# One input buffer of a fused layer norm and GELU: loaded in one transfer instead of four row transfers

## The chip, the cores and the metric

The kernel runs on one core of a Trainium2 chip. The metric is the device time of one execution in microseconds (us). Some executions of a kernel are over 1.5% slower than its fastest; they are said to be slow. A profile's span is some 1.8 us shorter than the time of the same execution, so times are compared with times and places in a profile with places in a profile.

Ratios are the mean time of one kernel's fast runs over that of the other's of the same rounds, so they are not quite the ratio of the medians that are quoted beside them. For the experiments, working them out again from the recorded times gives the ratios only if the first run of each list is left out. That run is the profiled one; it is counted in the medians.

## The reference

The input is 8192 rows of 2048 numbers in fp32, 67.1 MB. The output has the same size.

```python
mean = np.mean(x, axis=-1, keepdims=True)
var = np.var(x, axis=-1, keepdims=True)
normalized = (x - mean) / np.sqrt(var + eps)
out = gamma * normalized + beta
return 0.5 * out * (1 + np.tanh(np.sqrt(2 / np.pi) * (out + 0.044715 * out ** 3)))
```

## The kernel before

The rows are cut into 16 buffers (`B`) of 128 partitions with four rows each (`R`), 4.19 MB a buffer. There are five slots in SBUF (`SLOTS`). A buffer is loaded into a slot, overwritten there by its result and stored from there. SP, the sync engine, issues all loads, and before each it waits until the slot's former buffer has been stored. The engines wait for each other by semaphores, counters that one raises and another waits for; a transfer that has landed adds 16, or the multiple of it that the program asks for. The rows of one partition are contiguous in memory, so a whole buffer moves in runs of 32 KB, one for each partition, and a row transfer in runs of 8 KB.

```python
@block.sync
def _(sy):
    for b in range(B):
        s = slot(b)
        if stored(b):
            sy.wait_ge(s_store[s], stored(b))
        for q in range(R):
            if b == 0:
                sy.dma_start(out=xts[s][:, q:q + 1], in_=xg[0, :, q:q + 1]).then_inc(s_first[q], 16)
            elif b == SPLIT:                                   # SPLIT = 3
                sy.dma_start(out=xts[s][:, q:q + 1], in_=xg[b, :, q:q + 1]).then_inc(s_load[s], 16)
        if b not in (0, SPLIT):
            sy.dma_start(out=xts[s], in_=xg[b]).then_inc(s_load[s], 16 * R)
```

The vector engine (DVE) takes the statistics of each row. The first of a buffer waits for the load. In the order of its instructions the statistics of the next row come ahead of the scaling of this one:

```python
def stats(s, q, wait, count):
    ...
    for j in range(nsub):
        ins = ve.bn_stats(out=sts[:, q, j, :], in_=xr[:, j, :])
        if j == 0 and wait:
            ins._wait_ge(*wait)
            ...
...
for k in range(SLOTS * R):
    s, q = divmod(k, R)
    stats(s, q, (s_load[s], 16 * R) if q == 0 else None, k + 1)
    scale((q - 1) % R, k + 1)
```

The scalar engine (ACT) normalizes each row and later applies GELU to it, and it issues the stores: whole buffers, except for the last, which goes out row by row.

```python
ins = ac.activation(out=xt[:, q], in_=pss[i % 2], func=ACT.Gelu_apprx_tanh)._wait_ge(s_t, i + 1)
if by_row(b):                                                  # b == B - 1
    ins.then_inc(s_r, 1)
    ac.dma_start(out=og[b, :, q:q + 1], in_=xt[:, q:q + 1])._wait_ge(
        s_r, b + q + 1).then_inc(s_store[slot(b)], 16)
    ac.sem_inc(s_g, 1)
elif q == R - 1:
    ins.then_inc(s_r, 1)
    ac.dma_start(out=og[b], in_=xt)._wait_ge(s_r, b + 1).then_inc(s_store[slot(b)], 16)
    ...
```

Of the kernel before, what the change touches and what calls it, by code (L numbers as in the profile page):

```python
# [9 lines left out]

R = 4
SLOTS = 5
SPLIT = 3
K = 16


# [1 line left out]
def kernel(  # L18
# [19 lines left out]
    xg = xf.rearrange("(b p r) d -> b p r d", p=P, r=R)  # L38
# [8 lines left out]
    def sb(name, shape, dt):  # L47
        return pool.tile(shape, dt, name=name)

    xts = [sb(f"xt{s}", [P, R, d], f32) for s in range(SLOTS)]  # L50
# [17 lines left out]
    def sem(name):  # L68
        return tc.alloc_semaphore(name)

    s_first = [sem(f"first{q}") for q in range(R)]
    s_load = [sem(f"load{s}") for s in range(SLOTS)]
# [16 lines left out]
    def slot(b):  # L89
        return (b + SLOTS - 1) % SLOTS  # L90

    def row(p):
        return rows[p:p + 1, :, :d // K]

    def split(v):
        return v.rearrange("o (k f) -> o k f", k=K)
# [7 lines left out]
    def stored(b):  # L104
        return sum(16 * (R if by_row(c) else 1) for c in range(b) if slot(c) == slot(b))

    with tc.tile_critical(no_gpsimd_drain=True):  # L107
        with nc.Block(no_gpsimd_drain=True) as block:
# [7 lines that stand above are left out]
                    for q in range(R):  # L116
                        if b == 0:
                            sy.dma_start(out=xts[s][:, q:q + 1], in_=xg[0, :, q:q + 1]).then_inc(s_first[q], 16)
                        elif b == SPLIT:
                            sy.dma_start(out=xts[s][:, q:q + 1], in_=xg[b, :, q:q + 1]).then_inc(s_load[s], 16)  # L120
                    if b not in (0, SPLIT):
                        sy.dma_start(out=xts[s], in_=xg[b]).then_inc(s_load[s], 16 * R)

            @block.gpsimd
            def _(po):
# [18 lines left out]
            @block.vector  # L144
            def _(ve):
                def stats(s, q, wait, count):
                    xr = xts[s][:, q].rearrange("p (s f) -> p s f", f=FMAX)
                    for j in range(nsub):
                        ins = ve.bn_stats(out=sts[:, q, j, :], in_=xr[:, j, :])  # L149
                        if j == 0 and wait:  # L150
                            ins._wait_ge(*wait)
                            if wait[0] is s_load[s]:
                                ins.then_inc(s_load[s], -16 * R)
                    ins.then_inc(s_o, 1)
                    ve.bn_aggr(out=mvs[:, q], in_=sts[:, q])._wait_ge(s_o, count).then_inc(s_a, 1)  # L155

                def scale(q, count):
                    ve.tensor_tensor(out=zgs[q % 2], in0=yks[q % 2], in1=g_t,  # L158
                                     op=ALU.mult)._wait_ge(s_n, count).then_inc(s_z, 1)

                ve.memset(b_hl, 0.0).then_inc(s_m, 1)  # L161
                for q in range(R):
                    stats(slot(0), q, (s_first[q], 16), q + 1)
                    if q == 0:

                        ve.tensor_tensor(out=split(b_hl[32:33]), in0=row(32), in1=split(b_hl[32:33]),  # L166
                                         op=ALU.subtract)._wait_ge(s_c, 2).then_inc(s_m, 1)
                        ve.wait_ge(s_c, 3)
                    else:
                        scale(q - 1, q)  # L170
                ve.sem_inc(s_o, -R)
                ve.sem_inc(s_n, -(R - 1))
                with ve.Fori(0, (B - 1) // SLOTS):
                    for k in range(SLOTS * R):
                        s, q = divmod(k, R)
                        stats(s, q, (s_load[s], 16 * R) if q == 0 else None, k + 1)
                        scale((q - 1) % R, k + 1)
                    ve.sem_inc(s_o, -SLOTS * R)
                    ve.sem_inc(s_n, -SLOTS * R)
                scale(R - 1, 1)  # L180
# [102 lines left out]
```

## Time and profile before

| what | before |
|---|---|
| time, median of 3 (range) | 319.97 us (319.55 to 320.1) |
| span of the profile | 318.3 us |
| moved by DMA | 134.26 MB, mean 422 GB/s |
| stores issued in the steady part | every 19.36 us |
| last row store issued at | 309.36 us |

The first line below is from the page of the kernel before and gives busy time, share of the span and number of instructions of each engine (PE is the matmul engine, PEld its weight loads, POOL the GpSimd engine, which finishes the statistics of each row). The other two are from its lists of waits: who waited for whom, total us, how often, and the longest.

```profile
PE 244.3 (77%) x520; PEld 57.1 (18%) x520; DVE 247.3 (78%) x386; ACT 251.7 (79%) x132; POOL 110.4 (35%) x201
...
DVE sts L149 <- DMA xt<-in_x_dram: 31.2, 11, 3.8
...
SPq L122 <- DMA out_dram<-xt: 241.2, 11, 47.9
```

No engine is near its limit. The waits say that DVE waits for loads and that the loads wait for stores, which looks like a chain that could be shortened. (The "page" of a kernel is the summary of its profile.)

### The profile page before, as it was taken

The numbers are of one execution on the slowest core, as the hardware profiler recorded it, in microseconds if no ns is written. First come the engines' busy times: TensorE is split into PE (matmuls) and PEld (weight loads), VectorE is DVE, ScalarE is ACT, GpSimd is POOL, SyncE is SP. The second block draws the span as 40 slices with busy tenths as digits, with TensorE's granted clock in tenths as the row PEclk, the third lists the DMA queues.
The fourth block names the chain that finished last, engine by engine and source line by source line (L and its number), as shares of the span: only waits on it lengthen the run. The fifth ranks groups of instructions, "written<-read, shape, count | busy, mean of one in ns | idle before, by whom it ended". The sixth has DMA issues, their size and how long they took to land.

```text
span 318.3 us, 2090 instructions
## 1 busy us (share of the span) xinstructions
PE 244.3 (77%) x520; PEld 57.1 (18%) x520; DVE 247.3 (78%) x386; ACT 251.7 (79%) x132; POOL 110.4 (35%) x201
## 2 busy tenths in 40 slices
PE   2769999999999989687796868959689596877850
PEld 1212222222212112111121112212112111211110
DVE  3499999999999898786968968699686987869710
ACT  2769999999999989698696977969599595986860
POOL 1144444444444444232442333343342442324300
DMA  7999999999999999999999999999999999999994
GB/s 287 441 453 406 389 433 436 441 416 449 420 436 445 413 449 416 445 428 432 449 408 453 416 449 424 432 449 412 453 416 445 428 428 445 420 445 424 436 401 204
DMA packets 6002, 134.26 MB, mean 422 GB/s; under 512 B 704, under 2 KB 752, under 8 KB 752
## 3 DMA queue, kind: packets, MB, share of 16 engines
q1 hardware_dynamic: 3168, 67.11, 49.5%
q10 hardware_dynamic: 2832, 67.13, 49.0%
q14 instruction: 2, 0.02, 0.0%
HBM read 67.13 MB, written 67.11 MB: 422 GB/s over the span
## 4 chain that ended last, share of the span: by engine, by line
DMA 64%; ACT 14%; DVE 10%; POOL 5%; PE 3%; issue 1%; ACTq 0%; DVEq 0%; POOLq 0%; SPq 0%
DMA out_dram<-xt 31%; DMA xt<-in_x_dram 31%; ACT yk L195 9%; DVE sts L149 7%; ACT xt L202 4%; POOL ves L135 3%; DVE zg L158 2%; PE ps L220 2%; DMA rows<-in_gamma_dram 2%; POOL rss L137 2%; POOL nms L139 1%; DVE mvs L155 1%; PE ps L237 1%; ACT g_t L191 1%; ACTq L205 0%
## 5 line engine op out<-in xcount | busy, mean ns | idle before, releaser
L149 DVE BATCH_NORM_STATS2 sts<-xt 128x6 f32<-128x512 f32 x256 | 157.7, 679 | 33.0 <-DMA xt<-in_x_dram 31.2
L195 ACT ACTIVATE yk<-xt,nms,rss 128x2048 bf16<-128x2048 f32 x64 | 133.8, 2090 | 47.9 <-POOL nms L139 41.9
L237 PE MATMUL ps<-zg,ident 128*128 128x512 bf16 x256 | 120.8, 627 | 54.8 <-DVE zg L158 53.8
L233 PE MATMUL ps<-b_hl,ones_b 33*128 33x512 bf16 x256 | 120.6, 624 | 2.2 <-PEq L228 2.2
L202 ACT ACTIVATE xt<-ps 128x2048 f32<-128x2048 f32 x64 | 119.0, 1859 | 1.5 <-PE ps L237 1.5
L135 POOL TENSOR_SCALAR ves<-mvs 128x1 f32<-128x1 f32 x64 | 38.4, 600 | 178.4 <-DVE mvs L155 178.4
L158 DVE TENSOR_TENSOR zg<-yk,g_t 128x2048 bf16<-128x2048 bf16 x64 | 76.4, 1194 | 19.2 <-ACT yk L195 19.2
L237 PEld LDWEIGHTS ps<-zg,ident 128*128 128x128 bf16 x256 | 27.6, 130 | 148.0 <-DVE zg L158 112.7
L233 PEld LDWEIGHTS ps<-b_hl,ones_b 33*128 33x128 bf16 x256 | 27.0, 127 | 92.1 <-issue 88.4
L139 POOL TENSOR_SCALAR nms<-mvs,rss 128x1 f32<-128x1 f32 x64 | 35.7, 558 | 6.3
L137 POOL TENSOR_TENSOR rss<-ves,mhalf 128x1 f32<-128x1 f32 x64 | 35.3, 552 | 5.3
L155 DVE BATCH_NORM_AGGREGATE mvs<-sts 128x2 f32<-128x24 f32 x64 | 16.9, 264 | 2.2
L220 PE MATMUL ps<-rows,ones 1*128 1x512 f32 x8 | 7.2, 1076 | 6.1 <-DMA rows<-in_gamma_dram 6.1
L188 ACT ACTIVATE b_hl<-rows 1x2048 bf16<-1x2048 f32 x1 | 1.9, 1910 | 5.2 <-DMA rows<-in_beta_dram 5.2
L166 DVE TENSOR_TENSOR b_hl<-rows,b_hl 1x2048 bf16<-1x2048 f32 x1 | 2.3, 2282 | 2.5 <-ACT b_hl L189 2.5
L220 PEld LDWEIGHTS ps<-rows,ones 1*128 1x128 f32 x8 | 2.5, 326 | 9.2 <-DMA rows<-in_gamma_dram 6.1
L191 ACT ACTIVATE g_t<-ps 128x2048 bf16<-128x2048 f32 x1 | 1.9, 1878 | 2.1 <-PE ps L220 2.1
L184 ACT ACT_TABLE_LOAD x1 | 1.3, 1283 | 0.9 <-SPq L107 0.9
L189 ACT ACTIVATE b_hl<-rows 1x2048 bf16<-1x2048 f32 x1 | 1.9, 1908 | 0.0
L161 DVE MEMSET b_hl<- 33x1024 uint32 x1 | 0.9, 912 | 1.2 <-SPq L107 1.2
L126 POOL MEMSET ones<- 65x128 f32 x1 | 0.2, 202 | 0.5 <-SPq L107 0.5
L130 POOL TENSOR_SCALAR_AFFINE_SELECT ident<-ident 128x128 bf16<-128x128 bf16 x1 | 0.3, 295 | 0.1
(7 smaller groups left out, 0.9 us busy)
## 6 DMA issues: line engine op xcount, KB each, us to landing
out_dram<-xt ACTq DMA_DIRECT2D x15, 4096.0 KB, 33.3
xt<-in_x_dram SPq DMA_DIRECT2D x14, 4096.0 KB
xt<-in_x_dram SPq DMA_DIRECT2D x8, 1024.0 KB, 8.2
out_dram<-xt ACTq DMA_DIRECT2D x4, 1024.0 KB, 9.0
rows<-in_beta_dram ACTq DMA_DIRECT2D x2, 8.0 KB, 5.8
rows<-in_gamma_dram ACTq DMA_DIRECT2D x1, 8.0 KB, 5.1
```

The costliest lines, as they stand in the source:

```text
L135: po.tensor_scalar(out=ves[:, c], in0=mvs[:, k, 1:2], scalar1=float(eps), scalar2=1.0, op0=ALU.add, op1=ALU.mult)._wait_ge(s_a, k + 1).the ...
L137: po.tensor_tensor(out=rss[:, c], in0=ves[:, c], in1=mhalf, op=ALU.pow)._wait_ge(s_q, 2 * k + 1).then_inc(s_q, 1)
L139: po.tensor_scalar(out=nms[:, c], in0=mvs[:, k, 0:1], scalar1=rss[:, c], scalar2=-1.0, op0=ALU.mult, op1=ALU.mult)._wait_ge(s_q, 2 * k + 2 ...
L149: ins = ve.bn_stats(out=sts[:, q, j, :], in_=xr[:, j, :])
L155: ve.bn_aggr(out=mvs[:, q], in_=sts[:, q])._wait_ge(s_o, count).then_inc(s_a, 1)
L158: ve.tensor_tensor(out=zgs[q % 2], in0=yks[q % 2], in1=g_t, op=ALU.mult)._wait_ge(s_n, count).then_inc(s_z, 1)
L191: ac.activation(out=g_t, in_=pss[0], func=ACT.Identity)._wait_ge(s_tg, 1).then_inc(s_c, 1)
L195: ac.activation(out=yks[t % 2], in_=xts[slot(b)][:, q], func=ACT.Identity, scale=rss[:, q:q + 1], bias=nms[:, q:q + 1])._wait_ge(s_p, t + ...
L202: ins = ac.activation(out=xt[:, q], in_=pss[i % 2], func=ACT.Gelu_apprx_tanh)._wait_ge(s_t, i + 1)
L220: ins = pe.matmul(pss[0][:, cols(j)], lhsT=ones[64:65], rhs=rows[64:65, j * K // nsub:(j + 1) * K // nsub, :d // K], start=True, stop=True)
L233: ins = pe.matmul(ps[:, cols(j)], lhsT=ones_b, rhs=b_hl[:, cols(j)], start=True, stop=False)
L237: ins = pe.matmul(ps[:, cols(j)], lhsT=ident, rhs=zgs[k % 2][:, cols(j)], start=False, stop=True)
```

## The change

The row transfers of buffer 3 go. Its load becomes one transfer like all others, and with them goes the count of 64 on the load's semaphore, which was needed so that four transfers could add up to what one adds. Its intent is simpler code, with fewer and larger packets. What it puts at stake is what the row loads did: buffer 3 is the load that is in progress when the first store comes.

```diff
-SPLIT = 3
...
                         if b == 0:
                             sy.dma_start(out=xts[s][:, q:q + 1], in_=xg[0, :, q:q + 1]).then_inc(s_first[q], 16)
-                        elif b == SPLIT:
-                            sy.dma_start(out=xts[s][:, q:q + 1], in_=xg[b, :, q:q + 1]).then_inc(s_load[s], 16)
-                    if b not in (0, SPLIT):
-                        sy.dma_start(out=xts[s], in_=xg[b]).then_inc(s_load[s], 16 * R)
+                    if b:
+                        sy.dma_start(out=xts[s], in_=xg[b]).then_inc(s_load[s], 16)
...
-                                ins.then_inc(s_load[s], -16 * R)
+                                ins.then_inc(s_load[s], -16)
...
-                        stats(s, q, (s_load[s], 16 * R) if q == 0 else None, k + 1)
+                        stats(s, q, (s_load[s], 16) if q == 0 else None, k + 1)
```

## The prediction

> **What bounds the kernel now.** I read the page first: its slices, then its queue table.
>
> ```profile
> span 318.3 us, 2090 instructions
> ...
> DMA  7999999999999999999999999999999999999994
> ...
> DMA packets 6002, 134.26 MB, mean 422 GB/s; under 512 B 704, under 2 KB 752, under 8 KB 752
> ## 3 DMA queue, kind: packets, MB, share of 16 engines
> q1 hardware_dynamic: 3168, 67.11, 49.5%
> q10 hardware_dynamic: 2832, 67.13, 49.0%
> ```
>
> The DMA engines are at 90% or more in every slice but the first and the last, while DVE and ACT, the busiest engines, are at 78% and 79%. The bound is the sum of the bytes. The packet counts tell the queues apart. q1 has the loads: 14 whole buffers of 128 packets (32 KB each), 8 row loads of 128 packets (8 KB each) and 16 small packets for each of 22 transfers: 1792 + 1024 + 352 = 3168. q10 has the stores and the three small parameter loads, by the same count 2832. So one row of a partition is one packet, and the change makes packets of four times the size.
>
> Then I asked the trace for the queues in stretches: row loads alone (32 to 38 us), row loads of buffer 3 beside the first store (40 to 52), whole loads beside whole stores (140 to 280), row stores alone (304 to 314).
>
> ```profile
> DMA packets 347, 2.52 MB, mean 419 GB/s; under 512 B 40, under 2 KB 40, under 8 KB 40
> ...
> DMA packets 269, 5.07 MB, mean 423 GB/s; under 512 B 19, under 2 KB 19, under 8 KB 19
> ...
> q10 hardware_dynamic: 127, 4.03, 77.7%
> q1 hardware_dynamic: 141, 1.03, 21.4%
> ...
> DMA packets 2072, 60.56 MB, mean 433 GB/s; under 512 B 224, under 2 KB 224, under 8 KB 224
> ...
> q10 hardware_dynamic: 1037, 30.31, 50.2%
> q1 hardware_dynamic: 1035, 30.25, 50.0%
> ...
> DMA packets 564, 4.15 MB, mean 415 GB/s; under 512 B 66, under 2 KB 66, under 8 KB 66
> ```
>
> Two things are to be seen. The queues take turns packet by packet, so 8 KB packets against 32 KB packets give the store four fifths (4.03 MB against 1.03), and equal packets give equal halves. And the rate hardly depends on it: 8 KB packets cost 3% (419 to 423 against 433 GB/s).
>
> Last I read the chain that ended last and the times of issue, for how far the queues are from running dry.
>
> ```profile
> 68.81 26.64 DMA out_dram<-xt
> ...
> 95.47 33.66 DMA xt<-in_x_dram
> ...
> 138.03 35.69 DMA out_dram<-xt
> ...
> 36.05 0.36 ACTq L210 DMA_DIRECT2D out_dram<-xt  x1
> 52.44 0.34 ACTq L210 DMA_DIRECT2D out_dram<-xt  x1
> ...
> 309.36 0.34 ACTq L205 DMA_DIRECT2D out_dram<-xt  x1
> ```
>
> The chain says: a store lands, its slot's next load is issued, and the load lands 33.66 us later. But a buffer alone (4.19 MB) needs 9.7 us at 433 GB/s, or 19.4 at a half share. The rest is queueing behind earlier transfers, so a long step in this chain is not a latency that the change could shorten for the total. The buffers follow each other at 19.36 us (stores issued at 118.69, 138.03, 157.41), which is 8.39 MB at 433 GB/s.
>
> **What the Trainium skill says.** "DMA: Bandwidth & Descriptors", Queues, rings and completion order: each engine goes round robin between the queues it has work for, a packet at a time. The trace agrees, with 4:1 in bytes at 40 to 52 us, and here one packet is one partition's run. The same page, Where 436 GB/s comes from: a ceiling of 435.2 GB/s. The trace agrees: 433 in the steady part, so nothing is left to win there. The same page, Bandwidth: a 1 MB transfer alone makes 341 GB/s and 16 MB 425. The trace does not show that loss for the 1 MB row loads queued back to back (419), so I don't charge them for it. The same page, Anatomy of one DMA: a completion costs about 2 us after the data. Store 0's bytes end at about 52.3 us and it lands at 36.05 + 18.9 = 54.95, so 2.6 us here.
>
> **The change part by part.** Instructions on PE, DVE, ACT and POOL stay the same; on SP four issues become one. The DVE's wait counts 16 in place of 64. Nothing of that is on the path: SP issues its first eleven transfers by 6.4 us, and buffer 3 is touched after 60 us.
>
> (a) Buffer 3's bytes at a better rate. 4.19 MB take 10.0 us at 419 GB/s and 9.7 at 433: 0.3 us less. This is DMA time and counts in full, as DMA is the bound. The packets of q1 fall by 512 + 64 - 128 - 16 = 432, to 2736.
>
> (b) The shares while the first store runs. Summing q1 in slices of 1 us, the loads have moved 15.3 MB at 38.5 us, where the first store's packets start. Up to buffer 4 (five buffers, 20.97 MB) 5.7 MB are left, of which 1.5 MB belong to buffer 3. Now the store gets 80% and its bytes end at 52.3 us; buffer 4's load ends at about 70.5. With equal packets each queue has 433 / 2 = 216 GB/s: the store needs 19.4 us, to 57.9, and the loads 26.3, to 64.8. The store is 5.6 us later and the loads 5.7 us earlier, and the sum of bytes is unchanged. This costs nothing unless an engine runs dry.
>
> (c) Can it run dry? From the end of store 0's bytes to the first packet of the load that waits for it I count 2.6 us to land and some 2.5 to start (store 0 itself: issued at 36.05, first bytes at 38.5), so 5.1 us. Buffer 5's load can start at 57.9 + 5.1 = 63.0, and the load queue is empty only at 64.8. The margin is 1.8 us, where it was some 13. From then on both queues advance by 19.4 us a buffer and the margin stays. Should it be missed on some engine, the store queue has work (store 1 issued at 52.44, before store 0 ends at 57.9; later stores wait longer still), so that the engine writes instead of idling, and the stores catch up.
>
> (d) The end. The last load's bytes end at about 282; with the change at 276.4. After it come DVE, ACT and the row stores in an unchanged rhythm, so the last row is issued at about 303.8 in place of 309.36. It does not end earlier by that, because the store queue is fuller by the same bytes: 5.6 us at 216 GB/s are 1.2 MB more to write, at the full rate 2.8 us, and the reads that are gone earlier give just those 2.8 us back. One small loss: 5.6 us more of the run are stores alone, which the 1 us slices from 284 to 304 put at 8.5 MB in 20 us, or 426 GB/s; 5.6 us times (1 - 426 / 433) is 0.1 us. One small gain: the row stores now come at the last moment (309.36 + 2.5 = 311.9, where the row before ends at about 311.5), and later they will be waiting in the queue, perhaps 0.1 to 0.3 us.
>
> Sum: -0.3 + 0.1 - 0.1 = -0.3 us, so 319.97 becomes 319.7.
>
> **The rivals.** First, slower through the lost lead of the stores: the row loads of buffer 3 look like a device to let the first store through early, and (c) leaves 1.8 us of margin on an estimate that can be off by 2. If both queues had a gap in each round, say 0.5 us in ten rounds, the time would be 325. For it speaks only that the device is there. Against it speaks that a gap in the loads is filled by waiting stores; before, at 52 us, the store queue was empty (its bytes ended at 52.3, the next store was issued at 52.44) and the DMA rate in that microsecond did not fall. Second, faster by earlier loads: the DVE waits for loads 11 times, 31.2 us in all, 2.97 in each late round. Earlier loads remove one or two of these waits, and one would hope for 3 to 6 us. Against it: these waits are slack of an engine which isn't the bound, and the DMA has no gap behind them. The floor is 134.26 MB at 433 GB/s, 310.1 us, with 2.3 us before the first bytes and some 4 after the last: 316.4 of span, against 318.3 now. So over 2% faster is out of reach whatever happens. Third, the shares settle otherwise than by halves and the backlog of stores grows until a slot's turn-round starves DVE and ACT near the end: some 1 to 3 us more, 321 to 323. Against it: at 140 to 280 us the halves are exact (30.31 and 30.25 MB).
>
> **Range and chances.** The three runs before lie within 0.55 us, and my terms within 0.5. A bit more is left above, for the thin margin of (c), than below, where the floor stands. I expect 319.7 us, 8 times in 10 between 318.4 and 321.4. Over 2% is 6.4 us: faster 0.01, within 2% 0.95, slower 0.04.
>
> **What would show it.** Right: q1 with 2736 packets; equal bytes of both queues from 40 to 52 us; the first store landing 23 to 25 us after its issue (was 18.9); the last load issued some 5 us later than 252 and landing some 5 us earlier than 284; stores late in the run taking some 47 us to land in place of 36, loads some 21 in place of 32; the last row store issued at about 304; DMA still full in every slice but the ends. Wrong: slices of DMA below 9 in the middle, a mean rate under 430 GB/s between 140 and 280 us, or the last store issued later than 309.

## The result, and the profile after

The changed kernel takes 319.88 us (median of 6 runs, 319.77 to 320.07). The kernel before took 319.98 us in the same rounds (6 runs, 319.55 to 320.34). The ratio is 0.9998 with a 95% interval of 0.9985 to 1.001: the same.

The time has not moved, but the run inside has. These are lines of the page of the changed kernel: the span, the busy share of the DMA engines in 40 slices, and the two queues (q1 loads, q10 stores).

```profile
span 318.1 us, 2087 instructions
...
DMA  7999999999999999999999999999999999999994
...
q1 hardware_dynamic: 2736, 67.11, 49.4%
q10 hardware_dynamic: 2832, 67.13, 49.0%
```

The DMA engines are full in the same 38 slices as before, and q1 has the 432 packets fewer that were worked out. Next come the queues of the changed kernel in two stretches, from 40 to 52 us (the first pair of lines) and from 140 to 280 us (the other three): packets, MB, share of the engines' time.

```profile
q10 hardware_dynamic: 81, 2.65, 51.2%
q1 hardware_dynamic: 81, 2.13, 42.0%
...
DMA packets 2091, 60.65 MB, mean 433 GB/s; under 512 B 240, under 2 KB 240, under 8 KB 240
...
q10 hardware_dynamic: 1063, 31.16, 51.6%
q1 hardware_dynamic: 1028, 29.49, 48.8%
```

From 40 to 52 us the store and the load now take turns packet by packet (81 each), where the store had four fifths of the bytes. The bytes are not quite equal, 2.65 against 2.13 MB, because 16 of the load's 81 packets are small ones. The first store lands 24.8 us after its issue instead of 18.9. In the long middle part the rate is the same 433 GB/s, but the halves are no longer quite equal: the stores get a little more.

Last, the waits, the chain that ended last and the issue of the last row store, all of the changed kernel. In the chain each line has its start, its length and what it was.

```profile
DVE sts L146 <- DMA xt<-in_x_dram: 27.0, 9, 3.7
...
SPq L119 <- DMA out_dram<-xt: 246.9, 11, 55.6
...
210.76 44.72 DMA out_dram<-xt
255.49 24.38 DMA xt<-in_x_dram
...
305.19 0.34 ACTq L202 DMA_DIRECT2D out_dram<-xt  x1
```

Stores late in the run take 44.7 us from issue to landing, where they took 36.5, and loads take 24.4 us, where they took 32.1. The last load is issued 3.5 us later than before (255.49 against 251.99) and lands 4.2 us earlier (279.87 against 284.04). The last row store is issued 4.2 us earlier (305.19 against 309.36). The execution ends where it did, because the bytes to be stored are still in the queue.

### The profile page after: what moved, and what is told of

The parts are those of the page before. It is cut to its first block, busy times and chain, and to the rows that moved or that the text cites. A ratio compares the mean times of both kernels' runs of the same rounds, so it can differ in the third digit from the quotient of the medians.

```text
span 318.1 us, 2087 instructions
## 1 busy us (share of the span) xinstructions
PE 244.4 (77%) x520; PEld 57.3 (18%) x520; DVE 247.1 (78%) x386; ACT 251.5 (79%) x132; POOL 110.5 (35%) x201
## 4 chain that ended last, share of the span: by engine, by line
DMA 45%; DVE 19%; ACT 18%; POOL 9%; PE 3%; issue 2%; ACTq 0%; POOLq 0%; DVEq 0%; SPq 0%
DMA out_dram<-xt 28%; DMA xt<-in_x_dram 15%; ACT yk L192 13%; DVE sts L146 12%; DVE zg L155 5%; POOL ves L132 5%; ACT xt L199 4%; POOL rss L134 3%; PE ps L217 2%; DMA rows<-in_gamma_dram 2%; POOL nms L136 1%; DVE mvs L152 1%; PE ps L234 1%; ACT g_t L188 1%; ACTq L202 0%
## 5 line engine op out<-in xcount | busy, mean ns | idle before, releaser
L155 DVE TENSOR_TENSOR zg<-yk,g_t 128x2048 bf16<-128x2048 bf16 x64 | 76.4, 1194 | 19.4 <-ACT yk L192 19.4
L152 DVE BATCH_NORM_AGGREGATE mvs<-sts 128x2 f32<-128x24 f32 x64 | 16.8, 263 | 2.2
## 6 DMA issues: line engine op xcount, KB each, us to landing
xt<-in_x_dram SPq DMA_DIRECT2D x15, 4096.0 KB, 24.8
```

Of the source, the lines that this page charges most:

```text
L152: ve.bn_aggr(out=mvs[:, q], in_=sts[:, q])._wait_ge(s_o, count).then_inc(s_a, 1)
L155: ve.tensor_tensor(out=zgs[q % 2], in0=yks[q % 2], in1=g_t, op=ALU.mult)._wait_ge(s_n, count).then_inc(s_z, 1)
```

## The experiments

Three theories were to be told apart. The first is that of the prediction: full DMA engines set the time, and which queue is ahead has no price as long as one of them always has work. The second is that the lead of the stores is worth something, which may be why the row loads were put there. The third is that chains of waits set the time.

### Half a buffer not loaded (wrong result)

```diff
-                    if b:
+                    if b == 8:
+                        sy.dma_start(out=xts[s][:, 0:2], in_=xg[b, :, 0:2]).then_inc(s_load[s], 16)
+                    elif b:
                         sy.dma_start(out=xts[s], in_=xg[b]).then_inc(s_load[s], 16)
```

> Wrong result on purpose: of buffer 8 only the first two rows are loaded, 2.1 MB less, in the middle of the run. Theory (bytes are the bound): 2.1 MB at 433 GB/s are 4.8 us, so 315.1 us. Rival (a chain of waits or the computation is the bound): no change.

It took 314.92 us (4 runs, 314.81 to 315.14; ratio to the kernel before 0.9843, interval 0.9829 to 0.9857). The page shows the bytes and the unchanged mean rate:

```profile
DMA packets 5570, 132.16 MB, mean 422 GB/s; under 512 B 656, under 2 KB 704, under 8 KB 704
```

The engines have exactly as much to compute as before, and 2.1 MB less to move makes 5.0 us less, where the rate says 4.8. This fits bytes as the bound and rules out the computation alone. Taken alone it does not rule out a chain of waits through this load, which lands sooner too (20.2 us from issue to landing, where a whole load has a median of 24.6). Against a chain speak the DMA engines, which are full in 38 of 40 slices, and the run with three slots below, which shows what a binding chain looks like.

### A further DVE instruction for each row

```diff
                             if wait[0] is s_load[s]:
                                 ins.then_inc(s_load[s], -16)
+                        if j == 0:
+                            ve.bn_stats(out=junk, in_=xr[:, 0, :64])
```

`junk` is a new tile that nothing reads.

> The changed kernel with one more statistics instruction of 64 columns per row, result unused: some 0.2 us of DVE work for each of 64 rows, 13 us in all. Theory (the waits of DVE for loads, 27.0 us in all, are slack): the time stays within 1 us of 320, and the waits of DVE for loads shrink by some 8 to 13 us. Rival (these waits or the DVE are on the path): up to 13 us more.

It took 319.89 us (4 runs; ratio 0.9998, interval 0.9983 to 1.0012). The 64 added instructions took 208 ns each, 13.3 us together. The wait of DVE for loads in this run:

```profile
DVE sts L147 <- DMA xt<-in_x_dram: 21.2, 8, 3.7
```

The wait went from 27.0 to 21.2 us, by less than expected; the rest of the added work went into other gaps, as its wait for ACT ahead of the scaling, which went from 19.4 to 15.1 us. The time did not move by anything that can be told. So what DVE waits for loads is slack, and shortening it wins nothing.

### The first store in rows: the shares turned round

```diff
     def by_row(b):
-        return b == B - 1
+        return b in (0, B - 1)
```

The counts in the waits of the later stores rise by three to match.

> The changed kernel with the first store in four rows of 8 KB packets against whole loads of 32 KB packets: the shares of the kernel before turned round, one fifth for the first store. Theory: the loads up to buffer 4 end at about 57 us (65 in the changed kernel, 70 before) and the first store lands last of the three, at about 63 us (61, 55), buffer 5 is loaded from about 66 us, and the time stays at 320 us within 0.6, as the engines never run dry. Rival (an early landing of the first store is worth something): later than the changed kernel, by 2 us or more.

It took 319.78 us (5 runs, 319.38 to 319.82; ratio 0.9986, interval 0.9972 to 1.0). The queues from 40 to 52 us:

```profile
q1 hardware_dynamic: 143, 4.16, 81.0%
q10 hardware_dynamic: 143, 1.05, 20.7%
```

Again the queues take turns, 143 packets each, and now the load has four fifths of the bytes. The fourth row of the first store lands at 63.0 us (issued at 37.18, 25.8 us to land), against 60.8 in the changed kernel and 54.95 in the kernel before. Three quite different shares at the first store give three equal times. Here the lead of the stores is worth nothing.

### The last buffer stored whole, in both kernels

If the end of the computation comes earlier by 4 us and is hidden by the queue of stores, it has to come into view when that queue is taken away. The same edit in both kernels does it: the last buffer goes out in one store, which can't be issued until all of its rows are done.

```diff
     def by_row(b):
-        return b == B - 1
+        return False
```

In the changed kernel:

> The changed kernel with the last buffer stored whole, not by rows. This takes away the queue of stores at the end, so that the end of the computation sets the time. Theory: the last store is issued at about 305.2 us, starts 2.5 us later, needs 9.8 us and 4.5 us to complete: span 322, time about 324 us, 4 us more than with rows. It should be 4 us faster than the same edit of the kernel before, which shows that the change does end the computation earlier and that the queue of stores hides it. Rival (the change does nothing at all to the end of the computation): both edits give the same time.

In the kernel before:

> The kernel before with the last buffer stored whole. Theory: the last store is issued at about 309.4 us, starts at 311.9, needs 9.8 us and 4.5 us to complete: span 326, time about 328 us, 8 us more than with rows. Rival: the same time as the same edit of the changed kernel.

The changed kernel with this edit took 319.42 us (4 runs, 319.41 to 319.48), the kernel before with it 323.48 us (4 runs, 323.29 to 323.67). Both ran on the same chip in the same rounds. Below are the DMA slices and the issue of the last store, first of the changed kernel with the edit, then of the kernel before with it.

```profile
DMA  7999999999999999999999999999999999999986
...
304.42 0.34 ACTq L207 DMA_DIRECT2D out_dram<-xt  x1
```

```profile
DMA  7999999999999999999999999999999999999747
...
309.15 0.34 ACTq L210 DMA_DIRECT2D out_dram<-xt  x1
```

The difference is 4.06 us as expected: the 4 us were there all along, hidden in the queue. In the kernel before with the edit the DMA engines run empty before the last store (the slice with a 4, and 13 GB/s from 305 to 310 us). In the changed kernel only a small gap is left.

Both times were expected 4.5 us too high. I had charged the last store with 2.5 us to start, 9.8 us of bytes and 4.5 us to complete, 16.8 us. It took 11.1 us in the kernel before and 12.0 us in the changed one from issue to landing. The 2.5 us had been meant for a store that meets busy engines, the 4.5 us had been read at the end of a series of 8 KB packets.

### All loads by rows

```diff
-                        elif b == SPLIT:
+                        else:
                             sy.dma_start(out=xts[s][:, q:q + 1], in_=xg[b, :, q:q + 1]).then_inc(s_load[s], 16)
-                    if b not in (0, SPLIT):
-                        sy.dma_start(out=xts[s], in_=xg[b]).then_inc(s_load[s], 16 * R)
```

This edit is made in the kernel before, so the counts on the load's semaphore are 64.

> All fifteen later loads in four row transfers each, so 8 KB packets throughout: the row loads of buffer 3 multiplied by fifteen. Theory (the DMA engines are full from start to end and only bytes over rate count): 8 KB packets cost 0.3 us for each buffer's load alone, and up to 0.55 us if the store beside it is slowed too, so 15 buffers make +4 to +8 us: 324 to 328 us; the stores take four fifths while both queues have work, so a store should land in some 12 to 16 us after it starts and the stores wait for work. Rival (letting stores go ahead is a gain, and the row loads of buffer 3 were there for it): 320 us or less.

It took 331.39 us (4 runs, 330.55 to 332.14; ratio 1.0345, interval 1.0329 to 1.0361), 11.3 us more than the kernel before in the same rounds (331.39 against 320.11) and 3.4 us above the expected range. The lines are the rate from 140 to 280 us, the busy share of the DMA engines from 280 to 330 us in slices of 1.25 us, and the issue of the last row store.

```profile
DMA packets 5062, 59.64 MB, mean 426 GB/s; under 512 B 563, under 2 KB 563, under 8 KB 563
...
DMA  4999998318999999900000699999992999999960
...
324.33 0.34 ACTq L202 DMA_DIRECT2D out_dram<-xt  x1
```

The packets cost what the prediction said: 426 GB/s from 38 to 280 us, where the kernel before has 432, is 242 x (1 - 426 / 432) = 3.4 us, for some twelve buffers loaded in that time, 0.3 us for each. What I had left out is the end. With four fifths for every store the stores are always up to date (16.7 us to land) and all of the delay is with the loads. So the last loads come late (their bytes run to about 290 us, in the kernel before to about 281), no stores are left in the queue to be moved during the last computation, and the DMA engines stand empty for some 6 us from about 301 to 307 (33 GB/s) and in shorter holes beside that (362 GB/s from 280 to 300 us). So the time is not indifferent to the lead after all. It is only so while stores are left at the end.

### One more buffer by rows in the kernel before

That gives a new forecast for a small dose: the kernel before issues its last row store at 309.36 us, hardly before the engines would run out of stores, so a second buffer by rows must cost time, while a first one costs none.

```diff
-                        elif b == SPLIT:
+                        elif b in (SPLIT, SPLIT + 1):
...
-                    if b not in (0, SPLIT):
+                    if b not in (0, SPLIT, SPLIT + 1):
```

> The kernel before with buffers 3 and 4 loaded by rows, a second dose of what the change took away. Theory now (row loads hand the stores a lead, which costs nothing while stores are left in the queue at the end, and the kernel before has just used that up): the second store gets four fifths too, the last row store is issued about 5 us later than before, at some 314 us, the DMA engines stand idle ahead of it for 2 to 4 us, and the time is 322 to 324.5 us; another 0.3 us of it is the packet size. Rival (only the packet size costs): 320.4 us, last row store issued before 310.

Three fast runs took 321.66, 321.92 and 323.12 us (ratio 1.0079, interval 1.0055 to 1.0102, from the last two of them). Two of the three lie just below the expected range. A fourth, of 333.81 us, was slow and is not used. All that the DMA engines moved in the three microseconds from 295 to 298, one line for each, and the issue of the last row store:

```profile
DMA packets 5, 0.03 MB, mean 33 GB/s; under 512 B 4, under 2 KB 4, under 8 KB 4
DMA packets 1, 0.00 MB, mean 0 GB/s; under 512 B 1, under 2 KB 1, under 8 KB 1
DMA packets 0, 0.00 MB, mean 0 GB/s; under 512 B 0, under 2 KB 0, under 8 KB 0
...
313.87 0.34 ACTq L205 DMA_DIRECT2D out_dram<-xt  x1
```

The last row store is issued at 313.87 us, as expected. The hole is not right ahead of it but ahead of the last whole store, which is issued at 297.45 us: from about 294.5 to 298.3 us hardly anything moves. From 280 to 300 us the rate is 367 GB/s, where the kernel before has 434, which is 3.1 us of work missed. After the hole the engines keep busy (400 GB/s from 300 to 310 us, 418 from 310 to 318). Slices shorter than a packet are no guide there: 16 packets of 32 KB take 1.2 us at 433 GB/s, and slices of 0.5 us show them as full and empty in turn. The second dose costs 2.5 us (0.0079 of 320; 2.2 if the profiled run is counted), where the packets of one buffer make 0.3. It counts as the same speed by the 2% line, but is clear of the noise. The kernel before was near the edge: a last row store 4.5 us later costs it time, and the change took it 4 us away from there.

### All loads and all stores by rows

```diff
     def by_row(b):
-        return b == B - 1
+        return True
```

This is on top of all loads by rows, and the wait of each store counts rows.

> All loads and all stores by rows, so that every packet is 8 KB and the shares are equal. It separates the two parts of the 11.4 us that row loads for all buffers cost. Theory: the packet size now costs on both sides, some 420 GB/s in the middle in place of 433, so 326 to 329 us in all, but with equal shares the gap of 6 us in the DMA near the end is gone and the last row store is issued early enough to be queued. Rival (the cost is the packets alone, the shares do nothing): more than the 331.4 us, as there are still more small packets.

It took 328.29 us (4 runs, 327.33 to 328.47; ratio 1.0261, interval 1.0246 to 1.0276). The lines are the queues' sum from 140 to 280 us and the issue of the last row store.

```profile
DMA packets 8228, 59.81 MB, mean 427 GB/s; under 512 B 927, under 2 KB 927, under 8 KB 927
...
320.26 0.34 ACTq L202 DMA_DIRECT2D out_dram<-xt  x1
```

The time is in the expected range, but for another reason, so this counts as half a miss. The small packets cost less than I said (427 and not 420 GB/s, the same as with small packets on one side), and the gap at the end did not go, it broke up into holes between the last rows: the rate is 321 GB/s from 305 to 310 us and 266 from 310 to 320, with 8 KB packets and holes of up to some 1.7 us. A store by rows begins as soon as a row is done and not when its buffer is, so here too the stores are up to date all the time, with equal shares. This fits what went before, that it is the stores left at the end that count and not the shares as such. What it does tell for sure is that the rival falls: more small packets took 3.1 us less (in other rounds; by the ratios it is 2.7 us).

### Three slots in place of five

```diff
-SLOTS = 5
+SLOTS = 3
```

> The changed kernel with three buffers in place of five. Theory: now both queues run dry, because a buffer's round (load at half share 24.5 us, computation to the store's issue some 21 us, store 24.5 us) divided by three is 23 us, against 19.4 us of DMA work; at full rate while the other queue is empty it is 17 us, so some gaps: 325 to 350 us, DMA slices below 9 in the middle. It shows what running dry looks like and that five buffers are what keeps the lead of either queue without effect. Rival (the margin never mattered): 320 us.

It took 372.15 us (4 runs, 371.31 to 373.77; ratio 1.1646, interval 1.1619 to 1.1673), beyond the expected range. The lines are the DMA slices of its page and a piece of its chain.

```profile
DMA  7995979799998989989799798998988989889598
...
118.62 20.21 DMA out_dram<-xt
138.84 16.56 DMA xt<-in_x_dram
164.31 19.84 DMA out_dram<-xt
```

Here the chain is what it seems to be in the other profiles: a store of 20.2 us, a load of 16.6 and 8.9 us of computation make a round of 45.7 us for two buffers, 22.8 for one, and the DMA engines have gaps in most slices. My 23 us for a buffer came out, but by luck: of the terms in it the load took 16.6 us and not 24.5 and the store 20.2 and not 24.5, so that 31.7 and not 21 us of a slot's round (three times 22.8 us) went into computation and waiting for it. Sixteen times 23 us are already 368; the upper end of the range was added up wrongly. With five slots the same three terms (44.7, 24.4 and 8.9 us) are shared by four buffers, 19.5 us for one, which is what the bytes need.

### What is left of small packets

The loads of buffer 0 in two halves and the last stores in two halves, in the changed kernel:

```diff
-                        if b == 0:
-                            sy.dma_start(out=xts[s][:, q:q + 1], in_=xg[0, :, q:q + 1]).then_inc(s_first[q], 16)
+                        if b == 0 and q % 2 == 0:
+                            sy.dma_start(out=xts[s][:, q:q + 2], in_=xg[0, :, q:q + 2]).then_inc(s_first[q], 16)
...
-                        ac.dma_start(out=og[b, :, q:q + 1], in_=xt[:, q:q + 1])._wait_ge(
...
+                            ac.dma_start(out=og[b, :, q - 1:q + 1], in_=xt[:, q - 1:q + 1])._wait_ge(
...
```

> The changed kernel with buffer 0 loaded, and the last buffer stored, in two halves of 16 KB packets in place of four rows of 8 KB: what is left of small packets. Theory: 0.1 to 0.2 us less for each, so 319.5 to 319.8 us, hardly to be told from 319.9; the last half is issued at about 305.2 us and there is no gap before it, as the store queue still has the first half. Rival (the rows at the ends were needed): 2 us more or worse.

Five of six runs took 319.15 to 319.48 us, the sixth 322.57 for no reason that its clock shows. The median is 319.31, the ratio 0.9999 with an interval of 0.9968 to 1.003, which the one run widens, so a gain over the kernel before is not shown. Halves at the start with the last buffer stored whole:

> The two small gains put together: the changed kernel with buffer 0 loaded in halves and the last buffer stored whole. Theory: 319.1 to 319.5 us, below both kernels by 0.4 to 0.8 us. Rival: the gain of one uses up that of the other, 319.9.

It took 319.71 us (6 runs, 319.62 to 319.86; ratio 0.9991, interval 0.9979 to 1.0003). That is above the expected range. The two gains did not add up, and why is open; the sizes are those of the differences between rounds.

The best version of all that were run, by the ratio, is the changed kernel with its last buffer stored whole: 319.42 us against 320.11 for the kernel before (ratio 0.9979, interval 0.9964 to 0.9995). It needs the change: on the kernel before the same edit costs 3.4 us. At 0.2% it counts as the same speed.

## Why the prediction was right

**The number.** 319.7 us was expected and 319.88 measured, in a range from 318.4 to 321.4. The forecast of 0.3 us less is within the noise, so the number alone tells little, and what follows goes by the parts.

**The bound.** It held. 2.1 MB less took 5.0 us off, and 13.3 us of added DVE work took nothing. The steady rate was 433 GB/s before and after.

**(a), the packets, -0.3 us.** The size agrees with 0.3 us a buffer in the run with all loads by rows. In the change itself it can't be seen: the medians differ by 0.1 us, and the interval allows for -0.5 to +0.3 us.

**(b), the shares.** Shown: 81 packets of each queue beside 127 and 141 before. The bytes were not quite equal, 2.65 against 2.13 MB. The first store was to land at 60.5 us (57.9 and 2.6) and landed at 60.8. Here two errors cancelled. The prediction has its first bytes at 38.5 us, 2.5 us after the issue, but in the trace of the kernel before its first data packet starts at 39.8, 3.7 us after the issue. The bytes then took less than the 19.4 us of a half share, from about 39.8 to 57.5 us in the changed kernel.

**(c), running dry.** That no engine would stand idle was right, in the way named there: stores fill what the loads leave. The margin of 1.8 us did not stay as it was said to, though. A load takes 24.4 us late in the run, and the terms of (c), 2.5 to start, 19.4 at a half share and 2.6 to land, are 24.5. The sum fits better than its terms: of the last load, the trace shows the first data packet 3.5 us after the issue, the last one 17.9 us later and the landing 3.0 us after that. So a load meets no queue any more: no data packet of a load starts between 257.5 us, where the load before it ends, and 259.0, where the last one begins. The loads do have gaps, the stores take them (31.16 against 29.49 MB from 140 to 280 us), and the engines stay at 433 GB/s. The premise of the first rival came true without its price.

The numbers that followed, 21 us for a late load and 47 for a late store, were too far apart, with 24.4 and 44.7 measured. They had been found by moving both ends by 5.6 us, and a load of 21 us would have contradicted the 24.5 us of (c). The lead that the loads kept at the end is therefore 4.2 us and not 5.6, and the last row store was issued at 305.2 and not at 303.8.

**(d), the end.** Shown by taking the queue away: with the last buffer stored whole, the kernels differ by 4.06 us. The two small terms, 0.1 us each way, are below what the runs can tell (of the first, the 426 GB/s from 284 to 304 us are 424 in the trace, which changes nothing).

**The rivals.** Faster by earlier loads fell with the added DVE work. Slower through a lost lead fell with the change itself and with the turned shares. The third, shares other than halves, came true in a small measure (the 31.16 and 29.49 MB), but the 1 to 3 us that it was to cost did not come. What no rival had is the opposite: row loads in larger doses make the kernel slower by holding the last loads back (2.5 us for a second buffer, 11.3 for all, of which some 3.4 are the packets).

What the row loads of buffer 3 were meant for can't be told from these runs. In this kernel they change nothing in the time.

## What to carry to other kernels

Where two queues share full DMA engines, as here, a long wait in the chain can be a place in a queue, and moving one transfer ahead of another then only moves the wait, so look at the sum of the bytes and at both ends of the run before believing that a wait can be won. A lead was free here only while the queue that stayed behind had enough left to cover the last computation; test it by taking that queue away, as the last store did here. Packet sizes of two queues set how they share the engines, and here that was a far larger effect (four fifths for one side) than what the size did to the rate (1 to 3%).

## What the Trainium skill lacked or had wrong

- "DMA: Bandwidth & Descriptors", Queues, rings and completion order, has the round robin by packets but not what follows for two queues with runs of different size: bytes go in proportion to them. Here a packet in the profile was one partition's run, and 32 KB against 8 KB made 4.03 against 1.03 MB, turned round 1.05 against 4.16 MB.
- The same page, Bandwidth (Where 436 GB/s comes from), says that the HBM side, about 358 GB/s, binds for transfers between HBM and SBUF. Here, with one core at work, that did not bind: it moved 433 GB/s in loads and stores together over 140 us. The page's own note under Bandwidth keeps the 358 for two cores that both stream from one HBM domain; the passage lacks that condition. The ceiling of 435 in the same place agrees. Its table gives 341 GB/s for 1 MB, issued from GpSimd; 1 MB row transfers on SP and ACT, queued one behind the other, made 427 GB/s, loads and stores together. For a queued stream from SP the page has one rate, with rows of 4 KB, but none by packet size for loads and stores side by side: 426 to 427 GB/s with 8 KB packets here, 433 with 32 KB.
- The same page, Latency and other measured facts, gives some 0.6 us to the first byte for SP and ACT. Here the first data packet started some 0.8 us after the issue with empty engines (309.15 to about 310.0 us, the last store of the kernel before stored whole), and 3.5 to 3.7 us after it where the transfer met busy ones (the last load after the change, the first store before it). For the first byte the page doesn't tell these apart.
